# A planner that makes sixteen passes, and raises the urgency of what TensorE idled for

## The chip, the cores and the metric

The kernel runs on one core of a Trainium2 chip. The core has five engines with a queue of instructions each: TensorE (PE, matmuls and weight loads), VectorE (DVE), ScalarE (ACT), GpSimd (POOL) and SyncE (SP, which here only starts DMAs). The metric is the device time of one execution in microseconds (us), the median of several runs; lower is better.

## The reference

One layer of a hybrid encoder trunk, for 1024 frames of width 1024 in float32, with 256 memory tokens and an MLP of width 4096. Cut to what is computed:

```
h = rmsnorm(x, norm_mix_g)
proj = h @ w_in                                  # all columns of both branches and of the merge gates
# branch A: gated DeltaNet (GDN), 8 heads of 128, chunks of 64: causal conv + SiLU, l2norm of q and k,
#   a triangular solve in each chunk, then a scan over the chunks
y_a = (rmsnorm(gdn(...), gdn_norm_g) * silu(gz)) @ w_branch_gdn
# branch B: gated linear attention (GLA), 4 heads (keys 128, values 256), a scan over the chunks
y_b = (rmsnorm(gla(...), gla_norm_g) * silu(lr)) @ w_branch_gla
x = x + (sigmoid(gate_a) * y_a + sigmoid(gate_b) * y_b) @ w_out
h, m = rmsnorm(x, norm_xattn_g), rmsnorm(mem, norm_mem_g)
q, k, v = h @ xattn_wq, m @ xattn_wk, m @ xattn_wv          # 4 heads of 256
x = x + (softmax(q k^T / 16) v) @ xattn_wo
x = x + square(relu(rmsnorm(x, norm_mlp_g) @ mlp_w1)) @ mlp_w2
return rmsnorm(x, norm_final_g)
```

## The kernel before

**Arithmetic.** Activations lie transposed, 128 features by 512 frames to a tile. Every large product is made of three matmuls (`mm3`, lines 510, 512 and 514): each operand is split into a rounded high part, which ACT copies (`split`, L550), and the remainder, a subtraction on DVE or POOL (L551). In the profile the high and low parts are named `wop`, `whi`, `wlo` for weights (of `raw`, as loaded) and `A0a`, `A1b`, `B1a` and the like for activations; `pd` and `ps` are PSUM tiles.

**Stages, in order of time.** Phase 0 (to about 130 us) normalises the memory (`mT`, `acc`, `rs_o`), projects it to keys and values (`kv`), multiplies Wq and Wo with them once for all frames ("fold"), and stages the normalised x. A folded tile leaves PSUM in `gst` (on DVE at L718, on ACT at L732; a ring of three tiles), and a DMA from ACT's queue stores it to `Gd`. `t_sums` (L786 to L789) makes sums of blocks of x for a multiplication scheme with fewer products. GLA follows (130 to about 505 us; gate and decay `ex`, `qk`; `v` scaled by its norm at L1045), then GDN (to about 1100; substitution `pr` and `Pm` at L1250 and L1252, decay mask `dm` at L1165), the merge and the output projection, attention, the MLP (from about 1550), and the final norm. A norm takes sums of squares (`acc`, L619), a sum over partitions on TensorE (L593), a power on POOL (L541), three small operations and `rs_o` on DVE (L542 to L545), and a spread over rows on TensorE (L607).

**What sets the order.** The program is first written out in plain order and recorded. `Plan.make` then fixes the order on each engine. `depend` collects what each operation waits for: data, PSUM and ring slots. `forward` models the five engines: each one takes, whenever it is free, the ready operation with the smallest priority; TensorE takes the ready one that stands first in the program. Sums of two operands in SBUF ("flex") go to DVE or POOL, by which is free. Priorities come from `latest`: walking back from where the last pass put the matmuls, it gives each operation the latest start at which no matmul would come later. So a pass uses the matmul times of the pass before it. `make` runs ROUNDS passes and keeps the one whose modelled end is earliest; `apply` writes its order into the program. No time of the model is taken from the chip.

```
ROUNDS, TOP, PAD = 4, 228656, 128
...
        for _ in range(ROUNDS):
            start, order = self.forward(deps, self.latest(deps, at, max(at) + 5000))
            at, end = start, max(start)
            if best is None or end < best[0]:
                best = end, order, [o.eng for o in self.ops if o.flex], start
```

Of the kernel before, what the change touches and what calls it, by code (L numbers as in the profile page):

```python
# [51 lines left out]
def bcol(t, n):  # L52
# [7 lines left out]
           "Reciprocal", "StreamTranspose", "TensorScalarAffineSelect")  # L60
ENGINES = {mybir.EngineType.PE: "tensor", mybir.EngineType.DVE: "vector", mybir.EngineType.Activation: "scalar",
           mybir.EngineType.Pool: "gpsimd", mybir.EngineType.SP: "sync"}
ROUNDS, TOP, PAD = 4, 228656, 128
BAND = 300


# [81 lines left out]
class Plan:  # L148
# [135 lines left out]
    def forward(self, deps, prio):  # L284
# [84 lines left out]
        assert not any(left)  # L369
        return start, order  # L370

    def make(self):

        calls = set(self.calls)
        marks = deque(self.marks)
        n = 0
        for i, ins in enumerate(self.trace()):
            while marks and marks[0].at <= i:
                self.ops.append(marks.popleft())
            if ins.engine in ENGINES and ins.opcode in OPCODES:  # L380
                self.ops.append(Op(ins, i in calls))
        self.ops += marks
        deps = self.depend()
        t, at = 0.0, []
        for o in self.ops:
            at.append(t)
            if o.eng == "tensor":
                t += o.cost
        best = None
        for _ in range(ROUNDS):  # L390
            start, order = self.forward(deps, self.latest(deps, at, max(at) + 5000))
            at, end = start, max(start)
            if best is None or end < best[0]:
                best = end, order, [o.eng for o in self.ops if o.flex], start
        self.end, self.final = best[0], best[3]
        number, k = {}, 0
        for i, o in enumerate(self.ops):
            if o.eng != "mark":
                number[i] = k
                k += 1  # L400
        flex = iter(best[2])
        sums = {o.name: next(flex) for o in self.ops if o.flex}
        engines = [sums.get(ins.name) for i, ins in enumerate(self.trace()) if i in calls]
        return [[number[i] for i in q] for q in best[1].values()], engines, [o.opcode for o in self.ops if o.eng != "mark"]
# [1944 lines left out]
```

## Time and profile before

| | us |
|---|---|
| median of 3 runs | 2225.49 (2225.03 to 2226.25) |
| the profiled execution | 2225.38 |
| its span | 2223.4 |
| TensorE busy | 2163.1 (97%) |
| DVE busy | 1658.8 (75%) |
| ACT busy | 1100.1 (49%) |
| POOL busy | 187.5 (8%) |

The span is from the first to the last instruction; 1.98 us of the execution lie around it. Busy times of engines overlap. A row of a timeline gives start, duration, engine, line, operation, output and inputs with their shapes, the number of equal instructions that follow each other, and in brackets the idle time ahead of it and what ended that. A row of windows gives the busy time of each engine in a stretch, and the clock that TensorE was granted (PEclk, 1.00 is full). Line numbers are those of the kernel before; the changed kernel's lines are 29 higher from the new function on.

### The profile page before, as it was taken

The numbers are of one execution on the slowest core, as the hardware profiler recorded it, in microseconds if no ns is written. First come the engines' busy times: TensorE is split into PE (matmuls) and PEld (weight loads), VectorE is DVE, ScalarE is ACT, GpSimd is POOL, SyncE is SP. The second block draws the span as 40 slices with busy tenths as digits, with TensorE's granted clock in tenths as the row PEclk, the third lists the DMA queues.
The fourth block names the chain that finished last, engine by engine and source line by source line (L and its number), as shares of the span: only waits on it lengthen the run. The fifth ranks groups of instructions, "written<-read, shape, count | busy, mean of one in ns | idle before, by whom it ended". The sixth has DMA issues, their size and how long they took to land.

```text
span 2223.4 us, 32153 instructions
## 1 busy us (share of the span) xinstructions
PE 2163.1 (97%) x11552; PEld 1851.5 (83%) x11552; DVE 1658.8 (75%) x3016; ACT 1100.1 (49%) x2223; POOL 187.5 (8%) x218
## 2 busy tenths in 40 slices
PE   7899999999999999999999999999999999999996
PEld 7788988878898888888877888998888888888886
DVE  7835999797966957759558994559998778667756
ACT  6443655354554545445534443455665556544433
POOL 2100111002111111111000000000100000000011
PEclk8999999999999999999999999999999999999998
DMA  6852111213212212121177771235364446778742
GB/s 233 280 175 83 58 66 47 71 62 100 72 34 77 62 39 91 39 81 43 57 250 231 259 246 57 98 126 158 121 199 146 157 156 197 253 246 282 244 122 81
DMA packets 148463, 300.20 MB, mean 135 GB/s; under 512 B 15816, under 2 KB 22344, under 8 KB 148304
## 3 DMA queue, kind: packets, MB, share of 16 engines
q1 hardware_dynamic: 141504, 289.75, 40.0%
q10 hardware_dynamic: 6800, 8.42, 1.1%
q8 instruction: 90, 1.47, 0.3%
q14 instruction: 69, 0.57, 0.1%
HBM read 212.35 MB, written 85.75 MB: 134 GB/s over the span
## 4 chain that ended last, share of the span: by engine, by line
PE 63%; DVE 11%; ACT 1%; issue 1%; DMA 1%; POOL 0%; DVEq 0%; ACTq 0%; POOLq 0%
PE pd L512 14%; PE pd L514 14%; PE pd L510 14%; PE ps L512 5%; PE ps L514 5%; PE ps L510 5%; DVE acc L1146 2%; DVE Pm L1252 1%; DVE pr L1250 1%; PE ps L1285 1%; PE ps L582 1%; PE ps L1325 1%; PE ps L1342 1%; PE ps L1205 1%; PE ps L1332 1%
## 5 line engine op out<-in xcount | busy, mean ns | idle before, releaser
L550 ACT ACTIVATE wop<-raw 128x512 fp32r<-128x512 f32 (+1 forms) x444 | 297.2, 675 | 497.4 <-PE pd L514 225.4
L551 DVE TENSOR_TENSOR wop<-raw,wop 128x512 fp32r<-128x512 f32 (+1 forms) x402 | 288.7, 721 | 142.8 <-ACT wop L550 135.5
L550 ACT ACTIVATE whi<-raw 128x512 fp32r<-128x512 f32 x86 | 52.1, 625 | 99.2 <-PE pd L512 65.0
L1146 DVE SCALAR_TENSOR_TENSOR acc<-cin,convw,acc 128x1024 f32<-128x1024 f32 x72 | 92.4, 1284 | 2.6 <-ACT acc L1144 2.3
L510 PE MATMUL pd<-t,wop 128*128 128x512 f32 x220 | 86.7, 394 | 2.4 <-ACT t L550 2.4
L514 PE MATMUL pd<-t,wop 128*128 128x512 f32 x220 | 89.0, 404 | 0.0
L512 PE MATMUL pd<-t,wop 128*128 128x512 f32 x220 | 86.4, 393 | 0.2 <-DVE t L551 0.2
L510 PE MATMUL pd<-B1a,wop 128*128 128x512 f32 (+1 forms) x220 | 82.8, 376 | 0.0
L514 PE MATMUL pd<-B1a,wop 128*128 128x512 f32 (+1 forms) x220 | 82.5, 375 | 0.0
L551 DVE TENSOR_TENSOR wlo<-raw,whi 128x512 fp32r<-128x512 f32 x77 | 52.0, 688 | 36.1 <-ACT whi L550 34.0
L510 PE MATMUL pd<-A0a,whi 128*128 128x512 f32 x172 | 69.7, 405 | 0.0
L510 PE MATMUL pd<-A1b,whi 128*128 128x512 f32 x172 | 69.1, 401 | 0.0
L512 PE MATMUL pd<-A1a,whi 128*128 128x512 f32 x172 | 68.2, 397 | 0.0
L514 PE MATMUL pd<-A1b,wlo 128*128 128x512 f32 x172 | 68.0, 395 | 0.0
L512 PE MATMUL pd<-A1b,whi 128*128 128x512 f32 x172 | 68.0, 395 | 0.0
L514 PE MATMUL pd<-A1a,wlo 128*128 128x512 f32 x172 | 67.9, 395 | 0.0
L512 PE MATMUL pd<-A0b,whi 128*128 128x512 f32 x172 | 67.9, 394 | 0.0
L514 PE MATMUL pd<-A0a,wlo 128*128 128x512 f32 x172 | 67.8, 394 | 0.0
L510 PE MATMUL pd<-A1a,whi 128*128 128x512 f32 x172 | 67.6, 393 | 0.0
L512 PE MATMUL pd<-B0b,wop 128*128 128x512 f32 x172 | 67.2, 391 | 0.2 <-DVE B0b L551 0.2
L510 PE MATMUL pd<-A0b,whi 128*128 128x512 f32 x172 | 67.3, 391 | 0.0
L512 PE MATMUL pd<-A0a,whi 128*128 128x512 f32 x172 | 67.3, 391 | 0.0
(598 smaller groups left out, 6971.6 us busy)
## 6 DMA issues: line engine op xcount, KB each, us to landing
raw<-in_w_dram SPq DMA_DIRECT2D x120, 256.0 KB, 3.7
raw<-in_w_gdn_dram SPq DMA_DIRECT2D x64, 256.0 KB, 2.9
raw<-in_w_dram SPq DMA_DIRECT2D x32, 512.0 KB, 3.8
e<-ad SPq DMA_DIRECT2D x63, 256.0 KB, 4.5
ad<-q SPq DMA_DIRECT2D x45, 256.0 KB, 2.9
rawa<-ad SPq DMA_DIRECT2D x42, 256.0 KB, 5.0
A0b<-tgd SPq DMA_DIRECT2D x32, 256.0 KB, 5.3
ad<-acc SPq DMA_DIRECT2D x30, 256.0 KB, 2.4
```

Of the source, the lines that this page charges most:

```text
L510: nc.tensor.matmul(out, lh, rh, start=first and i == 0, stop=False)
L512: nc.tensor.matmul(out, lh, rl, start=False, stop=False)
L514: nc.tensor.matmul(out, ll, rh, start=False, stop=last and i == n - 1)
L550: nc.scalar.activation(hi, raw, AF.Copy)
L551: (lo_eng or nc.gpsimd).tensor_tensor(lo, raw, hi.bitcast(F32), SUB)
L582: self.nc.tensor.transpose(pt[:, i * P:(i + 1) * P], s, self.ident)
L1146: nc.vector.scalar_tensor_tensor(acc, cin[:, 1 + i:1 + i + T], cw[:, i:i + 1], acc, MUL, ADD)
L1205: nc.tensor.matmul(pt[:, i * P:(i + 1) * P], kc, kc, start=True, stop=True)
L1250: nc.vector.tensor_tensor(pr, X[:, c + 1:32, c:c + 1].broadcast_to([P, m, n]), Pm[:, c:c + 1, 0:n].broadcast_to([P, m, n]), MUL)
L1252: nc.vector.tensor_tensor(Pm[:, c + 1:32, 0:n], Pm[:, c + 1:32, 0:n], pr, ADD)
L1285: nc.tensor.matmul(pt[0:96, i * n:(i + 1) * n], PF[:, v + i, 0:96], Z, start=True, stop=True)
L1325: nc.tensor.matmul(py[:, 0:P], st["NT"][:, c, :], zh[h], start=True, stop=True)
```

## The change

ROUNDS goes from 4 to 16. After each pass a new function, `hurry`, goes through TensorE's operations in their modelled order. Wherever the model has TensorE idle for 150 ns or more ahead of one, it walks back over what arrived last for it, up to 40 (HURRY) steps, and adds the idle time to `boost` of each operation on the way, once per pass; to one that stood behind another operation of its own engine it adds it a second time. The next pass sorts by the latest start less `boost`, which is kept from pass to pass. The first pass is that of the kernel before. Nothing is computed otherwise, and the instructions stay the same; their order changes, and with it whether DVE or POOL makes a flex sum.

```diff
-ROUNDS, TOP, PAD = 4, 228656, 128
+ROUNDS, TOP, PAD, HURRY = 16, 228656, 128, 40
...
+    def hurry(self, deps, start, order, boost):
+
+        ops, before, seen = self.ops, {}, set()
+        for q in order.values():
+            before.update(zip(q[1:], q))
+        for i in order["tensor"]:
+            j = before.get(i)
+            idle = start[i] - (start[j] + ops[j].cost if j is not None else 0)
+            if idle < 150:
+                continue
+            k = i
+            for _ in range(HURRY):
+                held = [(start[j] + ops[j].cost + (ops[j].own if ops[j].eng == ops[k].eng and not ops[j].dma else ops[j].lat)
+                         + (ops[j].bytes / 300 if ops[j].dma else 0), j) for j in deps[k]]
+                if not held:
+                    break
+                t, j = max(held)
+                e = before.get(k)
+                if e is not None and start[e] + ops[e].cost > t and ops[k].eng != "tensor":
+                    boost[k] += idle
+                k = j
+                if k in seen:
+                    break
+                seen.add(k)
+                boost[k] += idle
...
-        best = None
+        best, boost = None, [0.0] * len(self.ops)
         for _ in range(ROUNDS):
-            start, order = self.forward(deps, self.latest(deps, at, max(at) + 5000))
+            last = self.latest(deps, at, max(at) + 5000)
+            start, order = self.forward(deps, [s - b for s, b in zip(last, boost)])
             at, end = start, max(start)
             if best is None or end < best[0]:
-                best = end, order, [o.eng for o in self.ops if o.flex], start
+                best = end, order, [(o.eng, o.cost) for o in self.ops if o.flex], start, list(boost)
+            self.hurry(deps, start, order, boost)
+        best = best[:2] + ([e for e, _ in best[2]],) + best[3:]
```

Three places of the new order follow: phase 0 (DVE and ACT), GLA and the end (POOL); numbers behind names tell tiles apart. First DVE in phase 0, between about 78 and 91 us of the profile before: evictions of folded tiles (`gst`), remainders of weights (`wlo`) and of x (`A1a`, `A1b`), and the sums of x. Before:

```order
L718 TENSOR_TENSOR gst_126_838<-pd_125_825,rmb_65_489 128x256
L551 TENSOR_TENSOR wlo_139_902<-raw_137_900,wop_138_901 128x1024
L718 TENSOR_TENSOR gst_126_838<-pd_125_825,rmb_65_489 128x256
L551 TENSOR_TENSOR A1a_13_196<-x_161_1050,A1a_13_196 128x512
L786 TENSOR_TENSOR x_161_1050<-x_161_1050 128x512 x3
L718 TENSOR_TENSOR gst_128_855<-pd_127_842,rmb_65_489 128x256
L786 TENSOR_TENSOR x_161_1050<-x_161_1050 128x512
L718 TENSOR_TENSOR gst_128_855<-pd_127_842,rmb_65_489 128x256
L718 TENSOR_TENSOR gst_130_872<-pd_129_859,rmb_65_489 128x256
L703 TENSOR_TENSOR kv_133_893<-pd_140_906,kv_133_893 128x256
L718 TENSOR_TENSOR gst_130_872<-pd_129_859,rmb_65_489 128x256
L787 TENSOR_TENSOR x_161_1050<-x_161_1050,x_75_559 128x512 x2
```

The same place on DVE in the changed kernel:

```order
L580 TENSOR_TENSOR wlo_139_902<-raw_137_900,wop_138_901 128x1024
L747 TENSOR_TENSOR gst_128_855<-pd_127_842,rmb_65_489 128x256
L580 TENSOR_TENSOR A1b_14_197<-x_161_1050,A1b_14_197 128x512
L747 TENSOR_TENSOR gst_128_855<-pd_127_842,rmb_65_489 128x256
L580 TENSOR_TENSOR A1a_13_196<-x_161_1050,A1a_13_196 128x512
L747 TENSOR_TENSOR gst_130_872<-pd_129_859,rmb_65_489 128x256
L732 TENSOR_TENSOR kv_133_893<-pd_140_906,kv_133_893 128x256
L747 TENSOR_TENSOR gst_130_872<-pd_129_859,rmb_65_489 128x256
L747 TENSOR_TENSOR gst_132_889<-pd_131_876,rmb_65_489 128x256
L580 TENSOR_TENSOR wlo_144_962<-raw_142_960,wop_143_961 128x1024
L747 TENSOR_TENSOR gst_132_889<-pd_131_876,rmb_65_489 128x256
L815 TENSOR_TENSOR x_161_1050<-x_161_1050 128x512 x2
```

Both halves of gst 126 now stand ahead of `wlo_139`, and the sums of x (L786, now L815) and L787 stand behind gst 132. In the last fence the rows between gst 132 and L815 (a remainder and an eviction of `kv`) follow in the order they had.

On ACT's queue at about 70 to 78 us, the stores `Gd2` of the folded tiles and the splits of weights (`wop`) and of x, before:

```order
L719 DMA Gd2_62<-gst_112_758 128x512
L550 ACTIVATE wop_138_901<-raw_137_900 128x1024
L550 ACTIVATE A1a_13_196<-x_161_1050 128x512
L719 DMA Gd2_62<-gst_114_775 128x512
L550 ACTIVATE A1b_14_197<-x_161_1050 128x512
L719 DMA Gd2_62<-gst_116_792 128x512
L550 ACTIVATE wop_143_961<-raw_142_960 128x1024
```

and in the changed kernel, on the same queue:

```order
L579 ACTIVATE A1a_13_196<-x_161_1050 128x512
L579 ACTIVATE wop_138_901<-raw_137_900 128x1024
L748 DMA Gd2_62<-gst_112_758 128x512
L748 DMA Gd2_62<-gst_114_775 128x512
L579 ACTIVATE A1b_14_197<-x_161_1050 128x512
L579 ACTIVATE wop_143_961<-raw_142_960 128x1024
L748 DMA Gd2_62<-gst_116_792 128x512
```

The stores of gst 112 and 116 are now issued behind a weight's split, where they stood ahead of it.

On POOL in GLA, between about 441 and 479 us, before (`rs_y` is a power, `raw` a sum of weight blocks, `ex` the score tile that is cleared):

```order
L541 TENSOR_TENSOR rs_y_663_4224<-vv_662_4222,mhalf_2_176 128x8
L1600 TENSOR_TENSOR raw_691_4367<-raw_692_4368,raw_691_4367 128x4x128
L992 MEMSET ex_716_4533 64x8x64
L1005 AFFINE_SELECT ex_716_4533<-ex_716_4533 128x512 x2
L541 TENSOR_TENSOR rs_y_762_4710<-vv_761_4708,mhalf_2_176 128x8
```

and in the changed kernel:

```order
L570 TENSOR_TENSOR rs_y_663_4224<-vv_662_4222,mhalf_2_176 128x8
L1626 TENSOR_TENSOR raw_691_4367<-raw_691_4367,raw_692_4368 128x4x128
L1627 TENSOR_TENSOR raw_691_4367<-raw_691_4367 128x4x128
L580 TENSOR_TENSOR wop_706_4459<-raw_691_4367,wop_706_4459 128x512
L1631 TENSOR_TENSOR raw_692_4368<-raw_692_4368,raw_691_4367 128x4x128
L1021 MEMSET ex_716_4533 64x8x64
L1034 AFFINE_SELECT ex_716_4533<-ex_716_4533 128x512 x2
L570 TENSOR_TENSOR rs_y_762_4710<-vv_761_4708,mhalf_2_176 128x8
```

Four sums of weight blocks and remainders came to POOL and one (L1600) went to DVE. At the end of the program, from about 2200 us, POOL's queue was (`acc` are the sums of squares of the final norm, `B1b` a half of its output):

```order
L2177 TENSOR_TENSOR B1b_3711_20438<-B1b_3711_20438,q_3750_20631 128x512
L619 TENSOR_TENSOR acc_3751_20647<-acc_3751_20647,q_3755_20669 128x256
L619 TENSOR_TENSOR acc_3714_20441<-acc_3714_20441,q_3752_20649 128x256
L619 TENSOR_TENSOR acc_3751_20647<-acc_3751_20647,q_3764_20705 128x256
L619 TENSOR_TENSOR acc_3751_20647<-acc_3751_20647,q_3766_20716 128x256
L541 TENSOR_TENSOR rs_y_3761_20696<-n_v_3760_20693,mhalf_2_176 128x2
L541 TENSOR_TENSOR rs_y_3775_20758<-n_v_3774_20755,mhalf_2_176 128x2
```

and is in the changed kernel:

```order
L648 TENSOR_TENSOR acc_3714_20441<-acc_3714_20441,q_3752_20649 128x256
L570 TENSOR_TENSOR rs_y_3761_20696<-n_v_3760_20693,mhalf_2_176 128x2
L648 TENSOR_TENSOR acc_3751_20647<-acc_3751_20647,q_3764_20705 128x256
L648 TENSOR_TENSOR acc_3751_20647<-acc_3751_20647,q_3768_20727 128x256
L648 TENSOR_TENSOR acc_3751_20647<-acc_3751_20647,q_3770_20738 128x256
L648 TENSOR_TENSOR acc_3751_20647<-acc_3751_20647,q_3772_20749 128x256
L570 TENSOR_TENSOR rs_y_3775_20758<-n_v_3774_20755,mhalf_2_176 128x2
```

The sum of `B1b` went to DVE, as did the additions of q 3755 and q 3766; the last three additions came from DVE, and the first power stands ahead of POOL's additions to acc 3751. On the whole POOL has 232 instructions for 223, and nine more of the flex sums. TensorE's own order differs in 1164 of its 10622 rows, by 1.4 places on the mean.

## The prediction

> **What bounds the kernel now.** I read the page first, for its span and its busy times.
>
> ```profile
> span 2223.4 us, 32153 instructions
> PE 2163.1 (97%) x11552; PEld 1851.5 (83%) x11552; DVE 1658.8 (75%) x3016; ACT 1100.1 (49%) x2223; POOL 187.5 (8%) x218
> ```
>
> TensorE is busy for 2163.1 of 2223.4 us, and the change neither adds nor removes a matmul. So about 60 us, the time in which TensorE is not busy, is all that a better order could ever win, plus what a half-speed clock costs. DVE (75%) is the next engine, with room on the whole and little in places. The view of TensorE's waits says for whom it waits.
>
> ```profile
> PE pd L510 <- DVE gst L718: 8.2, 5, 2.9
> PE ps L607 <- DVE rs_o L545: 7.9, 3, 4.2
> PE ps L593 <- DVE acc L619: 6.3, 2, 4.6
> PE ps L582 <- DVE v L1045: 4.7, 1, 4.7
> PE pd L510 <- ACT t L550: 2.4, 1, 2.4
> PE ps L999 <- DVE ex L977: 2.0, 2, 1.0
> PE pd L512 <- DVE A1a L551: 0.8, 1, 0.8
> PE ps L582 <- DVE qk L981: 0.8, 2, 0.4
> ```
>
> The columns are the total, the times and the longest. The waits are few and each has a place: the start (one each of acc and rs_o), the folding of Wq and Wo with the memory (gst), GLA (ex, v), the loads near 1184 us (t), one split near 1588 (A1a) and the end (acc, rs_o again). Windows then show how full TensorE and DVE are at these places, and that in GDN (the last row) TensorE has no idle time to win.
>
> ```profile
> core 0: us, PE busy (x) PEld busy (x) DVE busy (x) ACT busy (x) POOL busy (x), PEclk, DMA share, GB/s
> 60.00:93.00 33.00, 24.37 (x166) 22.11 (x165) 30.65 (x54) 13.67 (x19) 8.53 (x6) 0.95 0.79 252
> 93.00:130.00 37.00, 34.20 (x216) 29.86 (x215) 21.07 (x25) 19.93 (x28) 0.00 (x0) 1.00 0.87 278
> 468.00:503.00 35.00, 28.97 (x170) 23.78 (x169) 30.99 (x53) 20.56 (x40) 3.60 (x4) 0.99 0.13 45
> 550.00:600.00 50.00, 50.00 (x255) 42.20 (x254) 47.57 (x100) 27.38 (x70) 8.55 (x16) 1.00 0.24 73
> ```
>
> **Fold of Wq, 60 to 93 us.** DVE is busy for 30.65 of 33 us, and in the 37 us behind that for only 21.07. TensorE is idle for 8.6 of the 33 us. Next come rows of DVE's timeline from there, and three of TensorE's gaps (in brackets the idle time ahead, and its releaser).
>
> ```profile
> 60.84 1.09 DVE L718 TENSOR_TENSOR gst<-pd,rmb 128x256 f32<-128x256 f32 x3 [1.91 <-DMA Gd<-gst]
> ...
> 65.72 1.22 DVE L551 TENSOR_TENSOR wlo<-raw,wop 128x1024 fp32r<-128x1024 f32 x1
> 66.86 1.41 DVE L718 TENSOR_TENSOR gst<-pd,rmb 128x256 f32<-128x256 f32 x4
> ...
> 81.02 0.42 DVE L718 TENSOR_TENSOR gst<-pd,rmb 128x256 f32<-128x256 f32 x1
> 82.07 1.89 DVE L786 TENSOR_TENSOR x<-x 128x512 f32<-128x512 f32 x3
> ```
> ```profile
> 68.08 0.35 PE L510 MATMUL pd<-kv,wop 128*128 128x256 f32 x1 [2.94 <-DVE gst L718]
> 81.58 0.35 PE L510 MATMUL pd<-mT,wop 128*128 128x256 f32 x1 [1.74 <-DVE gst L718]
> 86.22 0.38 PE L510 MATMUL pd<-mT,wop 128*128 128x256 f32 x1 [1.54 <-DVE gst L718]
> ```
>
> An eviction of 0.42 us stands behind a weight's remainder of 1.22 us ahead of each of the first two gaps, and behind three sums (1.89 us) ahead of the third. By the order these evictions now go ahead of the remainders, and the sums L786 and L787 go behind the last gst, into the stretch where DVE is half idle. Taking 1.22 us from each of the first two gaps and the whole 1.54 of the third gives 4.0. What is late next is the ring of three gst tiles: the row at 60.84 shows DVE held 1.91 us by the store Gd<-gst, and the change puts one such store (of gst 112) behind a split on ACT's queue that itself waits for TensorE.
>
> ```profile
> 72.65 1.06 ACT L550 ACTIVATE wop<-raw 128x1024 fp32r<-128x1024 f32 x1 [1.41 <-PE pd L512]
> ```
>
> That takes back up to 1.06 + 0.33 us. I take **3.0**, with 0 and 8.2 (the whole wait) as ends.
>
> **The clock.** Behind the 2.94 us gap the granted clock is halved for 3.41 us. Windows of that length show what was ahead of it, and one that had no such effect (PEclk is the third column from the end).
>
> ```profile
> 65.48:68.89 3.41, 0.81 (x7) 0.84 (x8) 3.41 (x8) 1.21 (x2) 1.30 (x1) 1.00 0.70 217
> 68.89:72.31 3.42, 3.42 (x19) 3.42 (x18) 2.67 (x6) 1.89 (x3) 2.28 (x2) 0.50 0.96 320
> 79.12:82.54 3.42, 1.68 (x15) 1.50 (x14) 3.38 (x6) 1.06 (x1) 0.00 (x0) 1.00 1.10 334
> ```
>
> A window with 0.81 us of matmul is followed by one at 0.50; the window 79.12 to 82.54, with 1.68 us, is not. A slow window filled with matmuls (3.42 of 3.42) costs half its length, 1.7 us. The 2.94 us gap lies inside the first window, and 1.22 us less of it brings that window to 2.03: I add **1.7** for 68.89, with 0 as the other end (the windows lie elsewhere against the work once the start shifts). The Trainium skill's page "TensorE: Matmul & The Clock Gate" (Part 1: The HAM clock gate) says that the array drops to half clock after an idle window of about 3.4 us, in windows that run free of the kernel; the trace agrees on the length, but 0.81 us of work in the window did not keep the clock up. By the rule taken as fully idle windows the 68.89 row would not exist and 1.7 would be no gain.
>
> **GLA, 320 to 328 and 468 to 503 us.** A sum of this size on POOL and on DVE, from the second stretch:
>
> ```profile
> 465.88 1.68 POOL L1600 TENSOR_TENSOR raw<-raw,raw 128x512 f32<-128x512 f32 x1 [23.04 <-DVE wop L551]
> 465.71 0.69 DVE L1542 TENSOR_TENSOR ex<-ex,ex 128x512 f32<-128x512 f32 x1
> ```
>
> Four sums of 0.69 us leave DVE for POOL there and one comes back, 2.1 us in all, and products of the decay go ahead of weight remainders. Half of the waits for ex and qk quoted above lies here, 1.4 us, and half at 325 us, where the products go ahead as well. On POOL such a sum takes 1.68 us against 0.69, four of them 6.7 us, one behind the other in front of a weight, so a part can come back as a wait for that weight. The 4.7 us wait for v stays: the operations of its chain keep their order. The sums that leave DVE may bring the scan behind them forward too, but the trace has that one at TensorE's pace. I take **2.0** of the 2.8 us of waits, with 0 and 2.8 + 2.1 = 4.9 as ends. A rule that speaks against this: the Trainium skill's page "SBUF — State Buffer" (Who interferes with whom) says that a VectorE instruction with two SBUF inputs and a GpSimd instruction that reads SBUF shut each other out for a whole instruction. By it the four moved sums would free DVE of nothing, the term would be about 1 and the whole sum 6.3. In the two rows above, which overlap, DVE's sum kept 0.69 us; whom the other one holds up where DVE is full, no row here decides.
>
> **1588 us and the end.** The wait for A1a is 0.8 us by the view of waits, and its split now goes ahead of weight sums on ACT and DVE: **0.8**, ends 0 and 0.8. At the end:
>
> ```profile
> 2199.91 1.30 POOL L2177 TENSOR_TENSOR B1b<-B1b,q 128x512 f32<-128x512 f32 x1 [6.49 <-ACT q L2169]
> 2201.17 1.86 POOL L619 TENSOR_TENSOR acc<-acc,q 128x256 f32<-128x256 f32 x2
> 2203.09 0.61 PE L593 MATMUL ps<-ones,acc 128*128 128x1 f32 x4 [1.43 <-POOL acc L619]
> 2207.78 0.42 DVE L619 TENSOR_TENSOR acc<-acc,q 128x256 f32<-128x256 f32 x1
> 2208.26 1.02 PE L593 MATMUL ps<-ones,acc 128*128 128x1 f32 x4 [4.56 <-DVE acc L619]
> 2210.85 0.48 DVE L2179 SCALAR_TENSOR_TENSOR B1b<-A0b,cols,ps 128x256 f32<-128x256 f32 x1 [1.38 <-ACT q L2169]
> 2212.70 0.15 DVE L542 TENSOR_TENSOR rs_t<-rs_y 128x2 f32<-128x2 f32 x1
> 2213.59 1.20 PE L607 MATMUL ps<-ident,rs_o 128*128 128x128 f32 x4 [3.26 <-DVE rs_o L545]
> ```
>
> The 1.30 us sum leaves POOL, so the first sum over rows at 2203.09 comes up to 1.4 earlier. But the last three additions now run on POOL, 0.9 us each against 0.42. From n_v onward the last chain is no longer held to 2212.70 by five operations of DVE, though some still stand between its steps. I take **0.8**, ends -1.5 and 2.
>
> **What is worth nothing or less.** At the start the sums of the memory go ahead, but DVE has the same operations ahead of the sum that TensorE waits for, and it is full: 0, ends -1.7 and 1.7 (one half-clock window more or less). From 1100 to 1550 us the order on TensorE, ACT and SP is as it was, so the wait for t stays: 0. In GDN TensorE is busy 50.00 of 50 us, so every stall that a move makes there is a loss and none can be won. Five more of the pr and Pm operations go to POOL, net:
>
> ```profile
> L1252 DVE TENSOR_TENSOR Pm<-Pm,pr 128x192 f32<-128x192 f32 x5 | 1.8, 357 | 0.1
> L1252 POOL TENSOR_TENSOR Pm<-Pm,pr 128x192 f32<-128x192 f32 x3 | 1.8, 595 | 15.3 <-DVE pr L1250 15.3
> L1165 DVE TENSOR_TENSOR dm<-dm,tm 128x1024 f32<-128x1024 f32 x8 | 9.7, 1216 | 0.0
> ```
>
> The means are 357 and 595 ns, so that is 5 x 0.24 = 1.2 us on a serial chain, beside dense matmuls that cover it. Three products dm of 128x1024 (1.22 us on DVE) go to POOL as well, where twice the 1.68 us of 128x512 is 3.4: 2.1 more for each, 6.4 in all. I take **-1** for what shows through the cover; the ends are 0 and -(1.2 + 6.4) = -7.6.
>
> The sum is 3.0 + 1.7 + 2.0 + 0.8 + 0.8 - 1 = 7.3 us. The profiled execution took 2225.38 us (1.98 around its span), 0.1 from the median of 2225.49, so the forecast is **2218.1**.
>
> **Rivals.** (A) The waits are only renamed: TensorE waits for the gst store or for ACT where it waited for DVE, the clock windows stay, and GLA's chain takes back its part. For it speaks that DVE is already held 1.91 us by the store at 60.84; against it, that the sums L786 really leave a full engine. It leaves 0 to 3 us: 2222 to 2225. That the kept pass hardly differs where it matters comes to the same time: the wait for t, 2.4 us, is not touched at all. (B) More than the forecast: the whole of gst's 8.2, the slow window at 68.89 (1.7), 3 in GLA, 0.8 at 1588, 2 at the end and one slow window fewer at the start (1.7): 17.4 us, 2208. For it speaks that DVE has room right behind each gap; against it that ring and ACT come next. (C) Slower: the serial chain pr, Pm, dm in GDN outlasts its cover of matmuls. There DVE is busy 47.57 of 50 us, so that the chain has 2.4 us of room in each such stretch; from there on the 7.6 us above come whole: less 2.4 of room that is 5.2, and with nothing won elsewhere 2230.6. Against it: DVE gives up the work that POOL takes on.
>
> **How the numbers follow.** Forecast (2213 to 2222) 0.52, A 0.24, B 0.14, C 0.10. What a measurement of this kernel can tell from no change is about 0.2%, 4.5 us: faster means below 2221.0, slower above 2229.9. B and 0.50 of the forecast, with 0.02 of A, are faster: 0.66. Of C, 0.09 lies above 2229.9; the rest is 0.25. The range starts at B's 2208 and goes past A to where half of C's loss has come, 2228: it leaves out most of C and the half of B that lies lower.
>
> **What will show it.** The wait for gst falls from 8.2 below 5, and no half clock follows near 69 us; where a store or ACT takes gst's place, A is right. DVE's busy time between 60 and 93 falls by some 4 us and rises behind. The waits for ex and qk shrink, the one for v stays near 4.7. Windows from 550 to 1100 keep TensorE at 49.6 to 50.00 of 50 (else C). The last rs_o comes about 1 us earlier against the last matmul. The forecast is wrong if new half-clock windows appear, most likely near 80 us, where the window of 1.68 us of matmul is only 0.87 above one that did it.

## The result, and the profile after

| | before | changed |
|---|---|---|
| median, us | 2226.18 | 2223.02 |
| lowest and highest of 22 runs, us | 2223.49, 2230.76 | 2218.33, 2227.67 |
| the profiled execution, us | 2225.38 | 2219.6 |

The ratio is 0.9983, with a 95% interval of 0.9976 to 0.999: 3.8 us less (2.2 to 5.3), just under the bound of 0.2% that the prediction set. The forecast was 7.3 us. The profiled execution of the changed kernel lies 3.4 us under its median, so its trace shows one of the faster executions. First, from the page of the changed kernel, span and busy times, then its view of TensorE's waits (total, times, longest):

```profile
span 2217.9 us, 32158 instructions
PE 2160.8 (97%) x11552; PEld 1845.9 (83%) x11552; DVE 1665.4 (75%) x3007; ACT 1101.6 (50%) x2223; POOL 205.9 (9%) x227
```
```profile
PE ps L636 <- DVE rs_o L574: 6.6, 2, 4.2
PE pd L539 <- ACT mT L696: 6.4, 1, 6.4
PE pd L539 <- DVE gst L747: 5.7, 6, 1.5
PE ps L1305 <- issue: 4.3, 4, 1.8
PE ps L611 <- DVE v L1074: 4.2, 1, 4.2
PE ps L622 <- POOL acc L648: 3.8, 1, 3.8
...
PE ps L622 <- DVE acc L648: 2.5, 2, 2.2
PE pd L539 <- ACT t L579: 2.3, 1, 2.3
PE ps L611 <- DVE acc L1181: 1.8, 3, 1.2
...
PE ps L1027 <- DVE ex L999: 0.9, 1, 0.9
```

Most waits at the known places shrank: gst from 8.2 to 5.7, rs_o from 7.9 to 6.6, acc (DVE and POOL together) from 7.7 to 6.3, v from 4.7 to 4.2, ex from 2.0 to 0.9; qk and A1a have no row left. The wait for the first mT grew from 5.2 to 6.4. Two rows grew from 0.3 us each in the kernel before: L1305 (4.3 us) and L1181 (1.8 us). Both lie in GDN, where the prediction said that nothing can be won. The windows of the changed kernel that answer to those of the prediction, and three of 150 us each in GDN:

```profile
60.00:93.00 33.00, 27.63 (x198) 25.66 (x199) 31.84 (x54) 17.04 (x22) 7.57 (x5) 1.00 0.86 289
93.00:130.00 37.00, 34.58 (x206) 29.57 (x205) 21.83 (x27) 20.66 (x29) 0.00 (x0) 1.00 0.92 293
...
550.00:700.00 150.00, 148.47 (x865) 128.00 (x864) 109.44 (x232) 77.05 (x214) 28.10 (x37) 1.00 0.19 62
700.00:850.00 150.00, 147.88 (x865) 127.94 (x865) 109.75 (x238) 77.86 (x215) 28.27 (x35) 1.00 0.18 59
850.00:1000.00 150.00, 147.89 (x864) 127.97 (x863) 111.72 (x241) 74.66 (x201) 26.93 (x35) 1.00 0.19 62
```

The same three in the kernel before:

```profile
550.00:700.00 150.00, 149.74 (x874) 129.66 (x873) 109.36 (x244) 78.41 (x216) 25.90 (x36) 1.00 0.19 60
700.00:850.00 150.00, 149.66 (x869) 129.29 (x868) 109.31 (x242) 75.95 (x210) 22.24 (x33) 1.00 0.19 61
850.00:1000.00 150.00, 149.66 (x865) 129.21 (x865) 111.97 (x246) 75.36 (x203) 23.26 (x32) 1.00 0.20 62
```

From 60 to 93 us TensorE does 3.3 us more (27.63 for 24.37), at full clock throughout (1.00 for 0.95). In GDN it loses 1.3 to 1.8 us in each window, and POOL is busier by 2.2 to 6.0 us in each.

To put the whole span into one account I compare the times between matmuls of the same number (both kernels have 11552). That gives, for the two profiled executions:

| from matmul to matmul | place | before | changed | won |
|---|---|---|---|---|
| to 105 | start | 24.09 | 24.99 | -0.90 |
| 105 to 320 | memory, folds begin | 35.95 | 34.30 | 1.65 |
| 320 to 1007 | fold of Wq and Wo | 140.11 | 134.96 | 5.15 |
| 1007 to 2816 | GLA | 304.94 | 304.51 | 0.43 |
| 2816 to 3039 | GDN begins | 44.99 | 46.28 | -1.29 |
| 3039 to 6248 | GDN | 550.08 | 554.14 | -4.06 |
| 6248 to 6614 | merge, loads | 89.94 | 88.41 | 1.53 |
| 6614 to 11440 | attention, MLP | 1000.00 | 999.45 | 0.55 |
| 11440 to the end | last norm | 33.28 | 30.86 | 2.42 |

The sum is 5.48, the difference of the spans. The rows 2816 to 3039 and 6248 to 6614 come from the clock: the changed kernel's profiled execution has two half-clock windows at 495 to 502 us, where that of the kernel before has one at 502 to 506 us, and it has none at 1168 us, where that one has one.

### The profile page after: what moved, and what is told of

Its sections match the earlier page's. It is cut to its first block, busy times and chain, and to the rows that moved or that the text cites. A ratio compares the mean times of both kernels' runs of the same rounds, so it can differ in the third digit from the quotient of the medians.

```text
span 2217.9 us, 32158 instructions
## 1 busy us (share of the span) xinstructions
PE 2160.8 (97%) x11552; PEld 1845.9 (83%) x11552; DVE 1665.4 (75%) x3007; ACT 1101.6 (50%) x2223; POOL 205.9 (9%) x227
## 4 chain that ended last, share of the span: by engine, by line
PE 72%; DVE 10%; issue 2%; ACT 1%; DMA 1%; POOL 0%; SPq 0%; DVEq 0%; ACTq 0%; POOLq 0%
PE pd L541 16%; PE pd L539 16%; PE pd L543 16%; PE ps L541 5%; PE ps L539 5%; PE ps L543 5%; PE ps L611 2%; PE ps L1314 1%; DVE wop L580 1%; DVE acc L1175 1%; PE ps L1354 1%; PE ps L1305 1%; PE ps L1371 1%; PE ps L1234 1%; PE ps L1361 1%
## 5 line engine op out<-in xcount | busy, mean ns | idle before, releaser
L543 PE MATMUL pd<-A0b,wlo 128*128 128x512 f32 x172 | 67.8, 394 | 0.0
```

The lines of the kernel that those rows point to most:

```text
L543: nc.tensor.matmul(out, ll, rh, start=False, stop=last and i == n - 1)
```

## The experiments

All runs are made in one way: the kernel computes both plans, that of before (four passes, no `hurry`) and the changed one, and puts the order together from pieces: up to a time of the first plan, each engine's instructions are taken from plan 0 (before) or plan 1 (changed).

```diff
+    def splice(self, plans):
+        old, out, engs, done = plans[0][3], {}, dict(plans[0][2]), set()
+        for t, p in CUTS:
+            part = {i for i, s in enumerate(old) if s < t} - done
+            done |= part
+            for e, q in plans[p][1].items():
+                out.setdefault(e, []).extend(i for i in q if i in part)
+            engs.update((i, e) for i, e in plans[p][2].items() if i in part)
...
```

In the first four (gdn_old, gdn_sums, fold_only, gdn_only) plan 1's first pass started from where plan 0 had left the flex sums, so their plan 1 differs in detail from the changed kernel's, at the start and early in GDN. In the other eight it is exactly the changed kernel's. Line numbers in their rows are 30 higher than the changed kernel's (L747 is L777 there). No run separates the two parts of the change, sixteen passes and `hurry`. Times are medians; the kernel before had 2226.42 beside the first four, 2228.05 beside gdn_old2 to tail_only, 2226.99 beside gdn_sums2 to short_tail and 2227.04 beside fold_true.

**Which stage loses.** The changed order everywhere but in GDN; the folds alone; GDN alone.

```diff
+CUTS = ((200e3, 1), (504e3, 1), (1090e3, 0), (1e9, 1))   # gdn_old
+CUTS = ((200e3, 1), (1e9, 0))                            # fold_only
+CUTS = ((504e3, 0), (1090e3, 1), (1e9, 0))               # gdn_only
```

> The changed kernel, with the order of GDN (from 504 to 1090 us of the plan) taken from the plan of before, on all engines. The two traces put a loss of 4.1 us there (TensorE is 5.05 us ahead at 520 us and 0.96 ahead at 1100). If that loss comes from GDN's own order (either theory below), this kernel is about 4 us faster than the changed one: some 2219 where the changed one has 2223.0 and before 2226.2, and TensorE's gaps at the norm's and the inverse's places (1.3 at 587 us, 2.0 at 765 and at 920) are gone. Rival: DVE's chain in GDN cannot follow a TensorE that comes 5 us earlier, whatever the order; then the gaps stay and it is equal to the changed kernel within 1 us.

> The plan of before, with phase 0 (to 200 us of the plan) alone from the changed one. The traces put 5.9 us of gain there at 130 us (7.1 less 1.2 of a later first matmul). If it holds to the end: 2220 to 2221 where before has 2226.2. If GDN's chain eats what comes earlier: 2224 to 2226, with new gaps in GDN although its order is that of before.

> The plan of before, with GDN alone (504 to 1090 us) from the changed one. If the changed order itself loses there, whatever comes ahead of it: 4 us slower than before, about 2230. If the loss is only that DVE's chain cannot keep up with an earlier TensorE: equal to before within 1 us.

| | median | ratio | 320 to 1007 | 3039 to 6248 |
|---|---|---|---|---|
| gdn_old | 2219.86 | 0.9966 (0.9953 to 0.9979) | 134.71 | 550.03 |
| fold_only | 2221.48 | 0.998 (0.9972 to 0.9988) | 135.29 | 551.53 |
| gdn_only | 2231.27 | 1.0019 (1.001 to 1.0028) | 142.35 | 555.65 |

The columns with two numbers are stretches between matmuls in the run's profiled execution, as in the table above. GDN's new order alone makes the kernel slower, by 4.2 us. Without it the rest of the change wins 7.6 us. The 551.53 of fold_only hold a half-clock window at 1076 us, where no other trace has one, and the 555.65 of gdn_only one at 928 us.

**What in GDN loses.** Three theories stood: POOL's sums, at their new places, shut DVE out; TensorE's own new order loses; the serial chain can't follow a TensorE that comes earlier (the form that rival C takes if the folds win). POOL makes nine remainders of weights in GDN before and after, but six of them now stand in pairs at the end of a substitution, and three dm are new to it. For the first theory speaks the trace of the changed kernel; rows of its timeline around 756 us, from POOL, DVE, ACT and TensorE:

```profile
756.26 2.56 POOL L580 TENSOR_TENSOR wlo<-raw,whi 128x512 fp32r<-128x512 f32 x2 [12.22 <-ACT whi L579]
756.28 1.32 DVE L1281 TENSOR_TENSOR Pm<-Pm,pr 128x31 f32<-128x31 f32 x1
757.63 1.25 DVE L1283 STREAM_TRANSPOSE X<-Pm 128x1024 f32<-128x1024 f32 x1
763.86 1.07 ACT L1291 ACTIVATE PF<-X 32x512 f32<-32x512 f32 x1
765.04 0.43 PE L1305 MATMUL ps<-PF,NT 128*128 128x96 f32 x2 [1.82 <-issue]
```

In the kernel before the same step of the chain, with POOL idle:

```profile
756.27 0.19 DVE L1252 TENSOR_TENSOR Pm<-Pm,pr 128x31 f32<-128x31 f32 x1
756.50 1.25 DVE L1254 STREAM_TRANSPOSE X<-Pm 128x1024 f32<-128x1024 f32 x1
```

POOL began 0.02 us before DVE, and a product of 31 columns, 0.19 us by itself, ended only when POOL's first half did: 1.32 us. The transposition behind it, the copies to `PF` on ACT and TensorE's L1305 all come later; TensorE waits 1.82 us (the view names no releaser, but the last `PF` ahead ends at 764.93). With dm it is the same, here in the changed kernel at 585 us:

```profile
584.99 1.92 POOL L1194 TENSOR_TENSOR dm<-dm,tm 128x1024 f32<-128x1024 f32 x1
585.31 2.75 DVE L1181 SCALAR_TENSOR_TENSOR acc<-tg,acc 128x512 f32<-128x512 f32 x2
587.52 0.66 PE L611 MATMUL ps<-ident,acc 128*128 128x128 f32 x4 [1.17 <-DVE acc L1181]
```

Two operations of 0.68 us take 2.75 together, while POOL works on dm until 586.91, and TensorE waits 1.17 us for the first of them. That the sums themselves come later from POOL would be another way to lose. For the wlo it is not seen: in the view by tile nothing waits for the nine that POOL makes. For two of the dm ACT waits, 2.1 us in all, but it waits 2.7 us for them when DVE makes them (gdn_sums2 below). If the first theory holds, putting these nine sums back on DVE brings GDN back to 550 us; by the two others it stays at 554; and by the third the old order of GDN loses as well once the folds are faster.

```diff
-CUTS = ((200e3, 1), (500e3, 1), (1090e3, 0), (9e8, 1))   # gdn_old2
+CUTS = ((200e3, 1), (500e3, 1), (1090e3, 1), (9e8, 1))   # gdn_sums2, gdn_wlo2
+MOVED = (4662, 5858, 7054,                               # dm (gdn_sums2 only)
+         4911, 6107, 7303, 4908, 6104, 7300)             # wlo, both halves
...
+        for i in MOVED:
+            new[2][i] = "vector"
+            new[1]["gpsimd"].remove(i)
...
```

> The changed kernel, with nine sums of GDN put back from POOL to DVE (three products dm, and the two halves of three weight remainders wlo, these behind the chain's last transposes); every other instruction keeps its place. Theory L: POOL's sums shut DVE out (DVE's Pm at 756.28 takes 1.32 us instead of 0.19 while POOL's wlo runs, its acc at 585.31 takes 2.15 instead of 0.68 while POOL's dm runs), so the chain is late and TensorE waits: 2 to 3 us faster than the changed kernel, although DVE has 7 us more to do, the gap at 765 below 1.0. Theory O: TensorE's own order enters the inverse too early: the gaps at 765 and 920 stay at 2.0, and the time is that of the changed kernel or up to 2 us above it.

> Exactly the changed kernel's order in phase 0, GLA and from 1090 us of the plan on, and before's in GDN (500 to 1090). The four runs so far used for their changed parts a plan that began its first pass from other places of the sums, and so differs in detail. If GDN's order costs 4 us (they gave 4.2 and some 3.5): 3.5 to 4.5 us below the changed kernel, a ratio to before of 0.9962 to 0.9968. If those figures came from the other detail of that plan: 0.998, as the changed kernel.

> Exactly the changed kernel, with nine sums of GDN put back from POOL to DVE (three products dm in their place, the two halves of three weight remainders wlo behind the chain's last transposes). Theory L (POOL's sums shut DVE out): a ratio to before of 0.9955 to 0.9968 where the changed kernel has 0.9983, TensorE's gap at 587 gone and the ones at 765 and 920 at 0.9 instead of 2.0. Theory O (TensorE's own order in GDN): 0.998 to 0.999, gaps as they were; DVE has 7 us more to do.

> The changed kernel, with only the six halves of wlo put back to DVE; the three dm stay on POOL. By theory L the gaps at 765 and 920 fall to 0.9 (about 2.2 us) and the gap of 1.3 at 587 and two of 0.5 at 742 and 897 stay: 0.9970 to 0.9976, about 1.5 us above gdn_sums2. By theory O: 0.998 to 0.999.

| | GDN's order | on DVE again | median | ratio | 3039 to 6248 |
|---|---|---|---|---|---|
| gdn_old2 | before's | | 2217.24 | 0.9953 (0.9941 to 0.9965) | 549.99 |
| gdn_sums | changed | 3 dm, 6 wlo | 2219.85 | 0.9968 (0.9956 to 0.998) | 549.49 |
| gdn_sums2 | changed | 3 dm, 6 wlo | 2216.73 | 0.9963 (0.995 to 0.9976) | 549.38 |
| gdn_wlo2 | changed | 6 wlo | 2220.07 | 0.9971 (0.9959 to 0.9983) | 551.95 |
| the changed kernel | changed | | 2223.02 | 0.9983 (0.9976 to 0.999) | 554.14 |

The windows of gdn_sums2 show TensorE full again, and its row of waits what is left of L1305:

```profile
550.00:700.00 150.00, 149.73 (x873) 129.55 (x872) 111.91 (x244) 76.87 (x213) 23.92 (x33) 1.00 0.19 62
700.00:850.00 150.00, 149.35 (x871) 129.33 (x870) 110.67 (x244) 78.48 (x216) 23.57 (x33) 1.00 0.19 59
850.00:1000.00 150.00, 149.35 (x872) 129.34 (x871) 111.35 (x244) 75.88 (x205) 22.66 (x33) 1.00 0.19 62
```
```profile
PE ps L1335 <- issue: 1.9, 4, 0.6
```

The first theory holds. Six remainders on POOL, where they stand, cost 2.2 us (554.14 less 551.95), three dm 2.6 (551.95 less 549.38). These are differences of single traces; with before's order of GDN the stretch takes 549.91 to 550.16 in the eight traces that have no half-clock window in it, so they are far above what it varies by. The medians alone can't tell gdn_sums2, gdn_wlo2 and gdn_old2 apart, since their intervals overlap. In gdn_wlo2, with dm still on POOL, the wait for acc stays as it was:

```profile
587.08 1.92 POOL L1224 TENSOR_TENSOR dm<-dm,tm 128x1024 f32<-128x1024 f32 x1
...
589.60 0.66 PE L641 MATMUL ps<-ident,acc 128*128 128x128 f32 x4 [1.14 <-DVE acc L1211]
```

The waits for acc add up to 1.8 us in the changed kernel, so the way by which the three dm cost the rest of their 2.6 us is not shown. To the rest of GDN's new order are left the 1.9 us at L1335 (0.3 in the kernel before), which cost nothing net, since 549.38 is below the old 550.08. The third theory falls by the runs below: in start_gdn_old, with before's order of GDN, matmul 3039 comes 7.1 us earlier than in the kernel before, and the stretch still takes 550.08. (In gdn_old2's own trace it comes only 0.5 us earlier, so its 549.99 says little on this.) gdn_sums agrees with gdn_sums2 with the other plan 1. gdn_old2 is faster than the 0.9962 to 0.9968 that were expected.

**The start, GLA, the end, the folds.** The changed order with before's GDN and before's first 27.89 us; GLA alone; all from 1090 us on alone; 27.89 to 200 us alone.

```diff
+CUTS = ((27.89e3, 0), (500e3, 1), (1090e3, 0), (9e8, 1))   # start_gdn_old
+CUTS = ((200e3, 0), (500e3, 1), (9e8, 0))                  # gla_only
+CUTS = ((1090e3, 0), (9e8, 1))                             # tail_only
+CUTS = ((27.89e3, 0), (200e3, 1), (9e8, 0))                # fold_true
```

> As gdn_old2, with the first 28 us of the plan from before as well. The first matmul stood at 5.6 and 6.2 us where the start is before's and at 6.8 to 7.5 where it is the changed one; its order gives the first weight and the first memory tile later. Theory: this 1.2 us is on the path, so 1 to 1.5 us faster than gdn_old2. Rival: DVE is full until 24 us and TensorE waits for its sum there in any case: equal to gdn_old2 within 0.5 us.

> Before, with GLA alone (200 to 500 us of the plan) from the changed plan. The prediction's term was 2.0 us of gain: a ratio of 0.9991. The two traces give 0.0 between 300 and 465 us, -1.8 and +1.8 around 465 to 490, and 0.8 us lost to a second half-clock window behind 495: together 0 or a loss of up to 1 us, a ratio of 1.000 to 1.0004.

> Before, with all from 1090 us of the plan on from the changed plan. By the two traces 1.3 us at 1588 and 2.9 behind 2190: 4.2 us faster, 2222.0, a ratio of 0.998. By the prediction's terms (0.8 and 0.8) 1.6 us: a ratio of 0.9993.

> Before, with 28 to 200 us of the plan alone (the folds of Wq and Wo) from the changed kernel; the start is before's. The prediction's terms for the folds were 3.0 us and 1.7 us of clock. If the evictions that go ahead of remainders and sums are the cause: from matmul 320 to matmul 1007 (60 to 200 us) 134 to 136 us where before's order took 140.1 to 142.4 in four traces, the wait for gst below 6 us where it was 7.8 to 9.3, and a ratio of 0.9973 to 0.9982. If the gain came from the start's other order of loads and sums: no gain here, 0.9995 to 1.0005.

| | median | ratio | to 105 | 320 to 1007 | 1007 to 2816 | from 11440 |
|---|---|---|---|---|---|---|
| start_gdn_old | 2215.80 | 0.9943 (0.993 to 0.9956) | 24.54 | 134.22 | 304.48 | 30.86 |
| gla_only | 2225.92 | 0.9992 (0.9983 to 1.0) | 24.43 | 141.53 | 304.43 | 33.26 |
| tail_only | 2224.62 | 0.9986 (0.9977 to 0.9994) | 24.57 | 140.17 | 304.92 | 29.95 |
| fold_true | 2217.63 | 0.996 (0.9946 to 0.9974) | 24.15 | 134.99 | 304.95 | 33.28 |

*The folds* carry the gain: 27.89 to 200 us alone makes the kernel 8.9 us shorter (5.8 to 12.0), more than was expected, and in its trace the stretch of the folds takes 134.99. The run moves all of this stage, so which of its moves counts most is not separated. Its row of waits for gst:

```profile
PE pd L569 <- DVE gst L777: 4.7, 5, 1.3
```

*GLA* is worth 0.4 to 0.5 us in the traces, and 1.8 (0 to 3.8) by the ratio, where nothing or a small loss was expected. The gaps at 325 us (1.02 for ex, 0.43 for qk in the trace of before) are gone, but from 1007 to 2559 the time is 249.97 before, 249.94 after and 249.91 in gla_only. Smaller gaps of up to 0.24 us behind ex, S and v came in their place; all gaps of the stretch add up to 1.95 us before and 1.02 after, and where the other 0.9 us went the gaps don't show.

*The end* is worth 2.4 to 3.3 us in the last stretch, less some 0.5 before it (489.88 us before, 490.38 in tail_only, from matmul 9264 to 11440). By the ratio of tail_only it is 3.1 us, between the two values that were expected. A part of the spread goes with the clock: it is halved 17.4 us behind matmul 11440 in tail_only, 15.0 us behind it in the changed kernel.

*The start* costs. With before's first 27.89 us matmul 105 starts at 24.03 to 24.57 us (six traces of the last eight runs and of before, 24.30 on the mean); with the changed order at 24.99, 25.58, 26.76 and 27.63, on the mean 1.9 us later. These four come in the order in which the clock becomes full for the first time: at 10.72, 13.95, 17.27 and 18.50 us, where it is at 9.78 to 10.87 with before's start. Two rows of gdn_wlo2, the worst, show the change of pace, and one shows that in the changed kernel it lies much earlier:

```profile
17.95 0.41 PE L569 MATMUL pd<-mT,wop 128*128 128x256 f32 x1
18.56 0.28 PE L569 MATMUL pd<-mT,wop 128*128 128x256 f32 x1
```
```profile
10.79 0.28 PE L543 MATMUL pd<-mT,wlo 128*128 128x256 f32 x1
```

Where the clock is full at 10.72, as it is with before's start, 0.7 us are left (24.99 for 24.30); the rest of the 1.9 goes with the clock. Why it becomes full later in three of the four traces is not shown. The first matmul alone doesn't explain it: it comes at 6.41 us in the best of the four and at 5.52 and 5.77 in two of the others. On DVE a weight's remainder that the new order puts in front of the sums of squares is late too, here in gdn_wlo2 and in the changed kernel:

```profile
21.09 1.23 DVE L610 TENSOR_TENSOR wlo<-raw,wop 128x1024 fp32r<-128x1024 f32 x1 [2.94 <-issue]
```
```profile
18.44 1.22 DVE L580 TENSOR_TENSOR wlo<-raw,wop 128x1024 fp32r<-128x1024 f32 x1 [1.13 <-issue]
```

DVE stands idle ahead of it. The profile names no releaser, and what this remainder waits for was not separated. That start_gdn_old is faster than gdn_old2 fits this, but their intervals overlap.

**Can the end be cut further?** In the changed kernel the last additions run on POOL and the last two norms' small operations are interleaved on DVE:

```profile
2200.76 2.34 POOL L648 TENSOR_TENSOR acc<-acc,q 128x256 f32<-128x256 f32 x3 [0.64 <-DVE rs_t L571]
```
```profile
2203.15 1.01 PE L622 MATMUL ps<-ones,acc 128*128 128x1 f32 x4 [3.79 <-POOL acc L648]
2204.03 1.20 PE L636 MATMUL ps<-ident,rs_o 128*128 128x128 f32 x4
2207.65 1.20 PE L636 MATMUL ps<-ident,rs_o 128*128 128x128 f32 x4 [2.42 <-DVE rs_o L574]
```

short_tail is start_gdn_old with the last three additions on DVE and the last two chains one behind the other, in the order that `TAIL` lists.

```diff
+TAIL = (16718, 16727, 16736, 16745, 16703, ..., 16759, 16770)
...
+        engs.update((i, "vector") for i in TAIL if i in engs)
+        out["gpsimd"] = [i for i in out["gpsimd"] if i not in TAIL]
+        k = out["vector"].index(TAIL[0])
+        out["vector"] = out["vector"][:k] + list(TAIL) + [i for i in out["vector"][k:] if i not in TAIL]
```

> start_gdn_old (0.9943), with the end changed on DVE and POOL: the last three additions of squares are made by DVE behind each other (0.42 us each, 0.34 from start to start) and not by POOL (0.75 to 0.9), and the last two chains of the norm are no longer interleaved with outputs. If the chain ones -> n_v -> rs_o -> rows sets the end: the sum at TensorE 1.5 us earlier, the last rows 2 to 3 us earlier, 0.9931 to 0.9936. If the outputs that now stand behind the chain set the end: within 0.5 us of start_gdn_old.

It took 2215.17, 0.9955 (0.9942 to 0.9967). Its last rows come 2.3 us earlier against matmul 11440, as expected, and its last stretch is 29.41 us instead of 30.86. But the clock is halved 17.4 us behind matmul 11440 in it, 15.3 in start_gdn_old; in tail_only, with 17.4 as well and the end of the changed kernel, the stretch takes 29.95, so about 0.5 us is left for the new order of the end. Beside start_gdn_old's 0.9943 (0.993 to 0.9956), on another chip, no gain in time is shown. start_gdn_old and short_tail, with gdn_old2 beside them, are the best kernels of the study: by their ratios some 10 to 13 us under the kernel before and 6 to 9 under the changed one.

## Why the prediction was right, and where not

Direction and range held: 2223.0 lies between 2208 and 2228, and the interval of the ratio (0.9976 to 0.999) leaves out 1. The size did not: 3.8 us by the ratio for 7.3, so that the outcome fell just inside the 0.2% that had a chance of 0.25. That it lies in the band of rival A (2222 to 2225) is no merit of A, since the wait for gst really shrank; the gain came and half of it was given back elsewhere. (Of A only the remark on GLA's chain came true.) That the range held is in part luck: in the two profiled executions the folds with their clock gave 2.1 us more than forecast and the end 1.2 more, while GDN cost 3.1 more, GLA gave 1.6 less and the start took 0.9, and these errors cancel for the greater part. By the prediction's own terms:

- **Fold, 3.0, and clock at 68.89, 1.7.** Right in place, and the waits that the forecast named did shrink; together 5.15 us between matmuls 320 and 1007 in the profiled execution, plus 1.65 just ahead. gst fell from 8.2 to 5.7, not below 5 as forecast, and lies at 3.5 to 5.8 in the seven traces with these folds. DVE's load between 60 and 93 us did not fall by 4 us but rose (31.84 for 30.65): it is as full as before, and only the order on it is better. The half-clock window is at 67.9 to 68.9 us in all four traces with the old folds, and at no place between 43 and 490 us in five of the seven with the new ones. The other two (gdn_old2 and gdn_sums2) have one at 116 and 113 us, and there the folds take 138.42 and 138.24. In both a load comes late first: ACT's split of a weight block of Wv waits for it, the eviction of kv stands behind that split, and TensorE waits for kv (0.6 us in the other five). Two rows of gdn_old2:

```profile
114.01 1.06 ACT L609 ACTIVATE wop<-raw 128x1024 fp32r<-128x1024 f32 x1 [3.42 <-DMA raw<-in_wv_dram]
115.39 0.50 PE L569 MATMUL pd<-wop,kv 128*128 128x512 f32 x1 [3.09 <-ACT kv L761]
```

  So the gain of the folds is not certain in each execution: some 3.4 us of it went to this wait and its slow window. Both traces have the changed start; none of the three with before's start shows it.
- **GLA, 2.0.** Wrong: 0.4 in the traces. The waits that the view names shrank as forecast, but the step from a shorter wait to an earlier matmul failed. That the moved sums come back as other waits was in the prediction, as a part only.
- **1588 and the end, 0.8 each.** A1a's wait is gone, and the stretch from matmul 8604 to 9264 took 0.97 less in this execution (149.12 for 150.09), but 149.88 to 151.02 in the others with this order, so its worth stays open. The end was mis-sized: 2.4 in the last stretch, about 2 net. The forecast that the last rs_o comes 1 us earlier was too small: the rows behind it start 20.6 us behind matmul 11440 where they started 23.5 behind it. Which of the moves did it was not separated.
- **Start, 0, and the loads, 0.** The start was mis-sized: -0.9 in the profiled execution, -1.9 on the mean of four, for the greater part by a clock that becomes full later. The wait for t stayed, as forecast (2.4 and 2.3).
- **GDN, -1.** The largest error: -4.06. The ends (0 to -7.6) held it. The place was rival C's, and its sign came too (148.47 and 147.88 of 150 us are 49.5 and 49.3 of 50, under its 49.6), but its price was worked out from the wrong thing. The prediction priced the moved sums by their length on POOL, and held against C that DVE gives up the work that POOL takes on. In fact dm on POOL takes only 1.92 to 2.05 us (the forecast had 3.4); what costs is that DVE stands still beside POOL's sums, as the rows at 756 and 585 us show. Runs gdn_sums2 and gdn_wlo2 give the price: 2.6 us for three dm, 2.2 for six wlo. The six wlo were not in the forecast at all.

The prediction had the rule in hand. The Trainium skill's page "SBUF — State Buffer" (Who interferes with whom) says that whichever of the two begins first holds the shared port for its whole instruction and the other one blocks; it was weighed for GLA alone, and set aside since in one pair of rows DVE kept its 0.69 us. The trace of before had the rows that decide it:

```profile
84.01 2.96 POOL L787 TENSOR_TENSOR x<-x,x 128x512 f32<-128x512 f32 x2 [8.00 <-DVE x L786]
84.22 1.61 DVE L786 TENSOR_TENSOR x<-x 128x512 f32<-128x512 f32 x1
```

POOL began first, and a sum of 0.69 us took 1.61. In the pair that the prediction read, DVE had begun first (465.71 against 465.88) and POOL's sum was the one that took 1.68 instead of the 1.27 that a sum of the same line takes at 342.73. So the trace agrees with the rule in both directions.

**What stays open.** Single terms measured in time don't add up to the whole: folds -8.9, GLA -1.8, end -3.1, GDN +4.2 and start about +2 make -7.6 us, the changed kernel has -3.8. The intervals of the four ratios are 4 to 6 us wide, so this is no contradiction, but it isn't explained either. The late load of Wv, seen in two of four traces with the changed start, may be a part of it; no run tests that. The stretches of the traces, which do add up, are what the reading above rests on.

## What to carry to other kernels

A planner that moves two-input sums to GpSimd has to charge VectorE for the time in which the two overlap; a move that shortens DVE's list can lengthen a serial chain on it by nearly a whole GpSimd instruction (here a product of 0.19 us became 1.32 beside a sum of 1.30). Where one engine is full (149.7 of 150 us), an order has almost nothing to win there (0.7 us at best in these runs) and 4 to lose, so leave such a stage as it is and reorder only where TensorE has gaps. A wait that goes from the view of waits is a gain only if a matmul of the same number further on comes earlier.

## What the runs showed that was not expected

The half-clock windows start at another phase in each execution. In the profiled execution before, two windows, one behind the other:

```profile
21.11:24.52 3.41, 1.25 (x9) 1.09 (x10) 2.89 (x7) 3.17 (x8) 0.00 (x0) 1.00 1.04 407
24.52:27.93 3.41, 0.81 (x5) 0.72 (x4) 2.05 (x7) 3.41 (x7) 1.40 (x1) 0.50 0.86 347
```

A window with 1.25 us of matmul is followed by half clock, where the prediction's 1.68 was not. The first slow stretch begins at 24.52 here and at 27.78 in the changed kernel; in the traces that start with before's order it begins between 23.44 and 26.93. The window at 1168 us is absent from fold_true, whose order is before's from 200 us on, and at 502 us there are one or two of them. By the prediction's count a slow window filled with matmuls costs 1.7 us, so a part of the spread of 7 to 9 us in the runs of both kernels may be of this kind. The Trainium skill's page "TensorE: Matmul & The Clock Gate" (Part 1: The HAM clock gate) says that the windows run free of the kernel; the trace agrees with that.
